# Weight pieces that begin 32 to 256 bytes into their buffers, with later attention steps and two half banks at the end

## The chip, the cores and the metric

The kernel runs on one NeuronCore of a Trainium2 chip (core 0). The metric is the device time of one execution in microseconds (us). Work is done by TensorE (PE in the profile; its loads of the stationary operand are listed apart as PEld), VectorE (DVE), ScalarE (ACT), and by DMAs that SyncE (SP) issues. GpSimd (POOL) only sets a few small buffers.

## The reference

A two-layer encoder trunk on 256 tokens of width 1024, in float32. Both layers sit between two half-step SwiGLU FFNs; the first mixes tokens by gated linear attention (GLA), the second by differential softmax attention.

```python
for i in range(2):
    x = x + 0.5 * swiglu_ffn(rms_norm(x, g[i, 0]), w_gu[i, 0], w_down[i, 0])
    h = rms_norm(x, g[i, 1])
    x = x + (gla_mixer(h, ...) if i == 0 else diff_mixer(h, ...))
    x = x + 0.5 * swiglu_ffn(rms_norm(x, g[i, 2]), w_gu[i, 1], w_down[i, 1])

def swiglu_ffn(h, w_gu, w_down):          # w_gu 1024 x 5632, w_down 2816 x 1024
    gate, up = jnp.split(h @ w_gu, 2, axis=-1)
    return (jax.nn.silu(gate) * up) @ w_down
```

The weights of the four FFNs, of the input and of the output projections are some 177 MB in all, read once.

## The kernel before

**Pieces of weights.** `weight_plan` lists all weights as 169 pieces of up to 1 MB, in the order in which they are used. A piece is loaded by one DMA into a staging buffer (`prefetch`), and then split by `parts` into a high and a low half (both float32r) that stand side by side in a buffer of the pool `wpool`: ACT copies the high half, DVE subtracts it from the staged weights to get the low half (line 186). There are five such buffers of 16 KB in each partition. The activations are split in the same way: `x2` (a normalized input), `a2` (the FFN's inner activation), `o2` and `do2` (outputs of the two mixers). A product is made as high times high, high times low and low times high.

**Which operand stands still.** In most products the weights are the stationary operand, 128 x 128 at a time, and the activation moves past them. Three helpers issue the matmuls:

- `mm3` (lines 210 and 211), for the FFNs: one matmul moves 512 columns (both halves of `x2` or `a2`) past the high weights, the next moves 256 columns past the low weights. Each pair of lines is a pair of matmuls with two loads. A gate or up projection is 11 chunks of 2 banks of 8 such pairs; the four FFNs make 4 x 11 x 2 x 2 x 8 = 1408 pairs on `x2`. The down projections of the first three FFNs make 3 x 4 x 2 x 22 = 528 pairs on `a2`.
- `mm1` (lines 203 to 205): three matmuls of 256 columns, for the GLA's q and k and for the output projections (`ps_w`).
- `mm_tok` (lines 225 to 227): the activation stands still and the weights move, mostly 512 columns at a time ("wide" pieces): the GLA's v and g, the differential layer's q, k and v, and the last FFN's down projection (`ps_d` on those lines).

**Where things lie.** In the build before, the five weight buffers begin at byte 42,400 of each partition and lie 16,384 bytes apart; `x2` begins at byte 132,512, the `a2` of the FFNs at 160,992 or 165,088, `o2` at 201,440 and `do2` at 162,016. Within each buffer every 128- or 256-column operand begins a multiple of 512 bytes further on. Modulo 512 bytes, then, a weight operand minus an `x2` operand is always 0, and a weight operand minus an operand of `a2`, `o2` or `do2` is always 192.

**The order of the differential layer** is written out by hand in the string `ORDER`. An `h` is a quarter or half of a projection (some 12 matmuls of 512 columns, or 24 of 256); between them stand the steps of head pair c: `b` statistics of q and k (`qk_stats`), `n` their scaling and transposition (`qk_norm`, tiles `qkx`, `ps_f`, `qkn`), `s` the softmax of one head (`ps_sc`, `s`), `f` the transposition of the probabilities (`flip`, `ps_T`, `dT`), `a` the product with v (`attend`, `ps_do`, `do`), `o` the transposition of the result (`normalize`, `ps_doT`). Each engine runs its own instructions in the order of the build.

**The end.** `down_out` makes the last down projection in two halves of 512 output columns, each of them in two banks of 128 tokens. In the very last bank, the last two of 22 blocks are done as two halves of 256 columns, so that DVE can add the first half to the residual (line 445) and SP can send it out (line 448) while the second is multiplied:

```python
if not whole:
    mm_tok(ps, w, act, t, k0, nk, hs, skip_group_check=h == 1)
nc.vector.scalar_tensor_tensor(out=xt[:, t, ho], in0=ps[:, hs], ...)
nc.sync.dma_start(out[0, ts_, ho], xt[:, t, ho])
```

Of the kernel before, what the change touches and what calls it, by code (L numbers as in the profile page):

```python
# [11 lines left out]
F32 = mybir.dt.float32  # L12
# [6 lines left out]
P = 128  # L19
# [11 lines left out]
WW, WK = 512, 4  # L31

N_STAGE = 3
WARM = 8
# [22 lines left out]
def weight_plan(w):  # L57

    plan = []

    def cols(a, start, width=CW, times=1):
        plan.append((a[:, start : start + width], KD, width, times))

    def wide(a, c, nk=KD):

        for k0 in range(0, nk, WK):
            n = min(WK, nk - k0)
            plan.append((a[k0 * P : (k0 + n) * P, c * WW : (c + 1) * WW], n, WW, 1))

    def both(a, b):  # L70

        for k0 in range(0, KD, WK):
            plan.append((tuple(z[k0 * P : (k0 + WK) * P, :CW] for z in (a, b)), WK, WW, 1))

    def ffn(i, j):
        gu, down = w["ffn_w_gu"][i, j], w["ffn_w_down"][i, j]
        for c in range(FF // CW):
            cols(gu, c * CW)
            cols(gu, FF + c * CW)
        if (i, j) == (1, 1):  # L80
            for c in range(D // WW):
                wide(down, c, NFB)
            return
        for dc in range(D // CW):
            for k0 in range(0, NFB, KD):
                n = min(KD, NFB - k0)
                plan.append((down[k0 * P : (k0 + n) * P, dc * CW : (dc + 1) * CW], n, CW, 1))

    ffn(0, 0)
    gla = w["gla_w_in"][0]  # L90

    cols(gla, gla.shape[1] - 32, 32, 4)
    for kind, c in GLA_COLS.split():
        if kind in "qk":
            cols(gla, "qk".index(kind) * 512 + int(c) * CW)
        else:
            wide(gla[:, 1024:], "vg".index(kind) * 2 + int(c))
    for c in range(4):
        cols(w["gla_w_out"][0], c * CW)
    ffn(0, 1)  # L100
    ffn(1, 0)
    for kind, c in DIFF_COLS.split():
        a, c = w["diff_w_in"][0], int(c)
        if kind == "a":
            both(a[:, c * CW :], a[:, D + c * CW :])
        elif kind == "b":
            wide(a[:, 2 * D :], c)
        else:
            cols(a, 2 * D + c * CW)
    for c in range(4):  # L110
        cols(w["diff_w_out"][0], c * CW)
    ffn(1, 1)
    return plan
# [3 lines left out]
def trunk(ctx: ExitStack, tc: tile.TileContext, ins, out):  # L117
# [19 lines left out]
    def prefetch(n):  # L137
        while state["dma"] < min(len(plan), n + LOOK_DMA + 1):
            i = state["dma"]
            src, nk, width, _ = plan[i]  # L140
            srcs = src if isinstance(src, tuple) else (src,)
# [10 lines left out]
    def parts():  # L152

        i = state["split"]
        _, nk, width, times = plan[i]
# [63 lines left out]

    def mm_tok(ps, w, act, t, k0, nk, cs=slice(None), **more):  # L220

        ts_ = slice(t * P, (t + 1) * P)
        for wk in range(w.shape[1]):
            k = k0 + wk
            mm(ps[:, cs], lhsT=act[:, k, 0, ts_], rhs=w[:, wk, 0, cs], start=k == 0, stop=False, **more)  # L225
            mm(ps[:, cs], lhsT=act[:, k, 0, ts_], rhs=w[:, wk, 1, cs], start=False, stop=False, **more)  # L226
            mm(ps[:, cs], lhsT=act[:, k, 1, ts_], rhs=w[:, wk, 0, cs], start=False, stop=k == nk - 1, **more)  # L227

# [197 lines left out]
    def down_out(act, nk, coef, xt):  # L426

        for c in range(D // WW):
            cs = slice(c * WW, (c + 1) * WW)
            banks = [psA.tile([P, WW], F32, tag="A", name=f"ps_d{c}_{t}") for t in range(2)]  # L430
            for k0 in range(0, nk, WK):
                w = next_weights()
                for t, ps in enumerate(banks):
                    if k0 + WK < nk:
                        mm_tok(ps, w, act, t, k0, nk)
                        continue

                    ts_, whole = slice(t * P, (t + 1) * P), t == 0 or c == 0
                    if whole:
                        mm_tok(ps, w, act, t, k0, nk)  # L440
                    for h in range(2):
                        hs, ho = slice(h * CW, (h + 1) * CW), slice(c * WW + h * CW, c * WW + (h + 1) * CW)
                        if not whole:
                            mm_tok(ps, w, act, t, k0, nk, hs, skip_group_check=h == 1)
                        nc.vector.scalar_tensor_tensor(  # L445
                            out=xt[:, t, ho], in0=ps[:, hs], scalar=coef, in1=xt[:, t, ho], op0=ALU.mult, op1=ALU.add,
                        )
                        nc.sync.dma_start(out[0, ts_, ho], xt[:, t, ho])

    def first_group():  # L450

        n = Norm(0)
        with ExitStack() as xctx:
            xp = xctx.enter_context(tc.tile_pool(name="xin", bufs=1))
            x_tm = xp.tile([P, 2, D], F32, name="x_tm")
            src, nk, width, _ = plan[0]
            t0 = staged[0] = stage.tile([P, nk, width], F32, tag="stage", name="stage0")
# [631 lines left out]
```

## Time and profile before

| | before |
|---|---|
| device time, median of 3 runs | 1006.99 us (1005.82 to 1007.09) |
| device time of the profiled execution | 1007.02 us |
| its span, first to last instruction | 1005.1 us |
| TensorE busy, as the profile counts it | 995.3 us (99%) |
| VectorE busy | 745.3 us (74%) |
| ScalarE busy | 566.1 us (56%) |
| HBM traffic | 177 GB/s over the span |

A matmul's length in the profile is modelled and overlaps the next one's; how long one holds up the next is read from the starts of two that follow each other. The profiled execution is within 0.1 us of the median of the runs, so that a sum made against it holds for the runs too.

### The profile page before, as it was taken

Reading aid. Unit: us, or ns where it says so; the run is one execution under the profiler, and the core shown is the slowest. Engines: PE = TensorE matmul, PEld = TensorE weight load, DVE = VectorE, ACT = ScalarE, POOL = GpSimd, SP = SyncE. Lnnn points to the kernel's source line nnn. Section 1 sums busy time; section 2 is a strip of 40 time slices with the busy share of each in tenths; the row PEclk is TensorE's granted clock in tenths of the full one; section 3 lists DMA queues with packets and bytes.
Section 4 is the critical chain, followed back from the end, with each engine's and each line's share of the span. In section 5 each row is a group of like instructions: output and inputs, shape, how many; then the busy total and the mean of one; then the engine's idle time right before and its main releaser. Section 6 shows DMA issues by size and latency. Waiting matters only on the chain.

```text
span 1005.1 us, 14771 instructions
## 1 busy us (share of the span) xinstructions
PE 995.3 (99%) x5830; PEld 870.4 (87%) x5830; DVE 745.3 (74%) x1275; ACT 566.1 (56%) x946; POOL 1.4 (0%) x9
## 2 busy tenths in 40 slices
PE   8999999999999999999999999999999999999998
PEld 7888888898889888888888888888878998888886
DVE  6988756499977987774669787556989689777640
ACT  6756545298655765553456565435586576655430
POOL 0000000000000000000000000000000000000000
PEclk9999999999999999999999999999999999999999
DMA  9876453565322775655457565465663258655530
GB/s 285 262 234 201 160 186 121 171 218 196 127 84 84 252 250 170 197 158 178 158 182 257 176 201 165 140 224 160 205 203 103 67 194 272 204 168 186 171 126 22
DMA packets 166787, 178.87 MB, mean 178 GB/s; under 512 B 4579, under 2 KB 155550, under 8 KB 166718
## 3 DMA queue, kind: packets, MB, share of 16 engines
q1 hardware_dynamic: 166318, 177.71, 54.7%
q8 instruction: 46, 0.75, 0.3%
q10 hardware_dynamic: 400, 0.21, 0.1%
q14 instruction: 23, 0.19, 0.1%
HBM read 176.84 MB, written 1.06 MB: 177 GB/s over the span
## 4 chain that ended last, share of the span: by engine, by line
PE 68%; DVE 5%; ACT 2%; issue 1%; ACTq 0%
PE ps_u L210 12%; PE ps_g L210 12%; PE ps_d L210 8%; PE ps_g L211 6%; PE ps_u L211 6%; PE ps_d L211 4%; PE ps_d L225 2%; PE ps_d L227 2%; PE ps_d L226 2%; DVE w L186 2%; PE ps_s L677 1%; PE ps_w L203 1%; PE ps_w L204 1%; PE ps_w L205 1%; ACT w L186 1%; PE ps_g L225 1%
## 5 line engine op out<-in xcount | busy, mean ns | idle before, releaser
L186 DVE TENSOR_TENSOR w<-stage,w 128x1024 fp32r<-128x1024 f32 x332 | 384.3, 1197 | 35.4 <-ACT w L186 35.2
L186 ACT ACTIVATE w<-stage 128x1024 fp32r<-128x1024 f32 x332 | 327.0, 1035 | 53.4 <-PE ps_d L227 15.3
L210 PE MATMUL ps_g<-x,w 128*128 128x512 f32 x704 | 250.6, 398 | 0.9 <-ACT w L502 0.9
L210 PE MATMUL ps_u<-x,w 128*128 128x512 f32 x704 | 249.1, 396 | 0.0
L211 PE MATMUL ps_g<-x,w 128*128 128x256 f32 x704 | 197.7, 282 | 0.0
L211 PE MATMUL ps_u<-x,w 128*128 128x256 f32 x704 | 197.5, 280 | 0.0
L210 PE MATMUL ps_d<-a,w 128*128 128x512 f32 x528 | 186.7, 396 | 0.0
L210 PEld LDWEIGHTS ps_g<-x,w 128*128 128x128 f32 x704 | 132.5, 189 | 32.8 <-ACT w L502 1.2
L210 PEld LDWEIGHTS ps_u<-x,w 128*128 128x128 f32 x704 | 132.1, 188 | 31.2
L211 PE MATMUL ps_d<-a,w 128*128 128x256 f32 x528 | 148.9, 282 | 0.0
L211 PEld LDWEIGHTS ps_g<-x,w 128*128 128x128 f32 x704 | 133.5, 190 | 0.2
L211 PEld LDWEIGHTS ps_u<-x,w 128*128 128x128 f32 x704 | 133.0, 189 | 0.0
L210 PEld LDWEIGHTS ps_d<-a,w 128*128 128x128 f32 x528 | 99.2, 188 | 24.0
L211 PEld LDWEIGHTS ps_d<-a,w 128*128 128x128 f32 x528 | 99.2, 188 | 0.0
L321 ACT ACTIVATE x<-x,par 128x256 fp32r<-128x256 f32 x40 | 20.0, 506 | 119.8 <-DVE x L374 119.8
L250 ACT COPY half<-ps_u 128x256 f32<-128x256 f32 x88 | 32.8, 372 | 90.4 <-PE ps_u L211 88.4
L250 ACT COPY half<-ps_g 128x256 f32<-128x256 f32 x88 | 32.3, 371 | 83.1 <-PE ps_g L211 81.5
L251 DVE TENSOR_TENSOR up<-ps_u,half 128x256 f32<-128x256 f32 x88 | 36.8, 421 | 40.4 <-ACT half L250 40.3
L374 DVE SCALAR_TENSOR_TENSOR x<-ps_d,x 128x256 f32<-128x256 f32 x48 | 20.3, 423 | 61.0 <-PE ps_d L211 60.1
L251 DVE TENSOR_TENSOR gate<-ps_g,half 128x256 f32<-128x256 f32 x88 | 36.8, 421 | 38.3 <-ACT half L250 38.3
L225 PE MATMUL ps_d<-w,a 128*128 128x512 f32 (+1 forms) x90 | 35.2, 391 | 0.5 <-DVE xt L445 0.5
L226 PE MATMUL ps_d<-w,a 128*128 128x512 f32 (+1 forms) x90 | 35.1, 390 | 0.0
(241 smaller groups left out, 1331.7 us busy)
## 6 DMA issues: line engine op xcount, KB each, us to landing
stage<-in_ffn_w_gu_dram SPq DMA_DIRECT2D x86, 1024.0 KB, 5.2
stage<-in_ffn_w_down_dram SPq DMA_DIRECT2D x34, 1024.0 KB, 5.3
stage<-in_gla_w_in_dram SPq DMA_DIRECT2D x12, 1024.0 KB, 7.6
stage<-in_ffn_w_down_dram SPq DMA_DIRECT2D x12, 768.0 KB, 4.5
stage<-in_diff_w_in_dram SPq DMA_DIRECT2D x16, 512.0 KB, 4.7
stage<-in_gla_w_out_dram SPq DMA_DIRECT2D x4, 1024.0 KB, 5.7
stage<-in_diff_w_in_dram SPq DMA_DIRECT2D x4, 1024.0 KB
stage<-in_diff_w_out_dram SPq DMA_DIRECT2D x4, 1024.0 KB, 5.5
```

The source lines that it names most:

```text
L186: op()
L203: mm(ps, lhsT=w[:, k, 0, ms], rhs=act[:, k, 0, :], start=first, stop=False)
L204: mm(ps, lhsT=w[:, k, 0, ms], rhs=act[:, k, 1, :], start=False, stop=False)
L210: mm(ps, lhsT=w[:, wk, 0, ms], rhs=act[:, k, :, :], start=first, stop=False)
L211: mm(ps[:, 0:T], lhsT=w[:, wk, 1, ms], rhs=act[:, k, 0, :], start=False, stop=last)
L225: mm(ps[:, cs], lhsT=act[:, k, 0, ts_], rhs=w[:, wk, 0, cs], start=k == 0, stop=False, **more)
L226: mm(ps[:, cs], lhsT=act[:, k, 0, ts_], rhs=w[:, wk, 1, cs], start=False, stop=False, **more)
L227: mm(ps[:, cs], lhsT=act[:, k, 1, ts_], rhs=w[:, wk, 0, cs], start=False, stop=k == nk - 1, **more)
L250: nc.scalar.copy(h[:, b, :], ps[:, T:512])
L251: nc.vector.tensor_tensor(out=out_t[:, b, :], in0=ps[:, 0:T], in1=h[:, b, :], op=ALU.add)
L321: high = nc.scalar.activation(self.x2[:, d, 0, :], src, AF.Copy, scale=g)
L374: nc.vector.scalar_tensor_tensor(out=x[:, d, :], in0=ps[:, h * T : (h + 1) * T], scalar=coef, in1=x[:, d, :], op0=ALU.mult, op1=ALU.add,)
```

## The change

Four things change.

1. A buffer of `wpool` becomes 16,896 bytes, and a piece begins at an offset in it that depends on how it is used: 24 elements (96 bytes) for weights that stand still beside `x2`, 8 (32 bytes) beside `a2`, `o2` or `do2`, 64 (256 bytes) for wide pieces that move past `x2`, 16 (64 bytes) for those that move past `a2`. The two narrow v pieces of the differential layer (256 columns, which also move past `x2`) get 96 bytes. The size and number of all splits and weight loads stay the same.
2. The memory kept for DMA descriptors shrinks from 16 KB to 8 KB in each partition, which makes room for the larger buffers.
3. In `ORDER`, twelve steps stand one quarter later (`n0`, `b1`, `n1`, `f0`, `s10`, `s11`, `a0`, `n2`, `s20`, `s21`, `a1`, `f2`) and two more stand two quarters later (`f1`, `o0`); the other ten stay (`s00` and `s01`, for one, now follow `n0` after one quarter where it was two).
4. In `down_out`, the very last bank becomes two tiles of 256 columns for all 22 blocks.

In the build after, the weight buffers begin at byte 34,208 and lie 16,896 bytes (33 x 512) apart; `x2` begins at 126,880, `a2` at 155,360 or 159,456, `o2` at 195,808 and `do2` at 156,384. Modulo 512 bytes the difference of a weight operand and the activation that it meets is:

| | before | after |
|---|---|---|
| weights stand still, `x2` moves | 0 | 96 |
| weights stand still, `a2`, `o2` or `do2` moves | 192 | 224 |
| wide weights move past `x2` | 0 | 256 |
| wide weights move past `a2` | 192 | 256 |

```diff
+BESIDE_X, BESIDE_A, WIDE_X, WIDE_A = 24, 8, 64, 16
+W_PAD = 128
...
-h h h h h h b0 h h n0 b1 h h s00 s01 n1 h h h f0 h s10 s11 h h f1 b2 a0 n2 h s20 s21 o0 h a1 h h b3 h f2 h n3 o1 a2 s30 s31 h h o2 hold
+h h h h h h b0 h h h n0 b1 h s00 s01 h n1 h h h f0 h s10 s11 h b2 h n2 a0 h f1 s20 s21 h a1 o0 h b3 h h f2 n3 o1 a2 s30 s31 h h o2 hold
...
-        w = split[i] = wpool.tile([P, nk, 2, times * width], FR, tag="w", name=f"w{i}")
+        n = nk * 2 * times * width
+        whole = wpool.tile([P, 2 * KD * CW + W_PAD], FR, tag="w", name=f"w{i}")
+        w = split[i] = whole[:, shift : shift + n].rearrange("p (k h c) -> p k h c", h=2, c=times * width)
...
-            banks = [psA.tile([P, WW], F32, tag="A", name=f"ps_d{c}_{t}") for t in range(2)]
+            banks = [[psA.tile([P, WW], F32, tag="A", name=f"ps_d{c}_{t}")] for t in range(2)]
+            if c == D // WW - 1:
+                banks[1] = [psA.tile([P, CW], F32, tag="A", name=f"ps_d{c}_1_{h}") for h in range(2)]
...
-    nc = bacc.Bacc("TRN2", target_bir_lowering=False, num_devices=1)
+    nc = bacc.Bacc("TRN2", target_bir_lowering=False, num_devices=1, dynamic_dma_scratch_size=8192)
```

What the steps look like on TensorE, at three places. First, the transposition of head pair 0's probabilities (`ps_T0`, `ps_T1`) in the middle of the differential layer's v projection (`ps_db0_0`, first token block). Before:

```order
L227 MATMUL ps_db0_0_6802<-w125_6537,x2_4_5895 128x512
L955 MATMUL ps_T0_6816<-cst_81,s0_0_6701 128x128 x4
L225 MATMUL ps_db0_0_6802<-w126_6646,x2_4_5895 128x512
L226 MATMUL ps_db0_0_6802<-w126_6646,x2_4_5895 128x512
L227 MATMUL ps_db0_0_6802<-w126_6646,x2_4_5895 128x512
L225 MATMUL ps_db0_0_6802<-w126_6646,x2_4_5895 128x512
L955 MATMUL ps_T1_6822<-cst_81,s1_0_6734 128x128
L226 MATMUL ps_db0_0_6802<-w126_6646,x2_4_5895 128x512
L955 MATMUL ps_T1_6822<-cst_81,s1_0_6734 128x128 x3
L227 MATMUL ps_db0_0_6802<-w126_6646,x2_4_5895 128x512
```

After (all lines of the file are 4 to 6 further on; the `ps_db0_0` group above ends before them):

```order
L232 MATMUL ps_db0_0_6802<-w126_6610,x2_4_5895 128x512
L233 MATMUL ps_db0_0_6802<-w126_6610,x2_4_5895 128x512
L231 MATMUL ps_db0_0_6802<-w126_6610,x2_4_5895 128x512
L232 MATMUL ps_db0_0_6802<-w126_6610,x2_4_5895 128x512
L233 MATMUL ps_db0_0_6802<-w126_6610,x2_4_5895 128x512
L959 MATMUL ps_T0_6837<-cst_81,s0_0_6701 128x128 x4
L959 MATMUL ps_T1_6843<-cst_81,s1_0_6734 128x128 x4
L231 MATMUL ps_db0_1_6849<-w125_6537,x2_4_5895 128x512
```

The transpositions stood between the two quarters of `ps_db0_0` and stand behind the second one now. Second, the product of head pair 1 with v (`ps_do1`) and the transposition of head pair 0's result (`ps_doT0`), between quarters of the last q and k projection (`ps_da3`). Before:

```order
L226 MATMUL ps_da3_0_7030<-w128_6797,x2_4_5895 128x512
L227 MATMUL ps_da3_0_7030<-w128_6797,x2_4_5895 128x512
L989 MATMUL ps_do1_7138<-dv_tm0_6847,dT1_6940 128x128 x2
L1006 MATMUL ps_doT0_7108<-cst_81,do_7006 128x128 x4
L989 MATMUL ps_do1_7138<-dv_tm0_6847,dT1_6940 128x128 x6
L225 MATMUL ps_da3_1_7172<-w127_6666,x2_4_5895 128x512
L226 MATMUL ps_da3_1_7172<-w127_6666,x2_4_5895 128x512
```

After, behind the next quarter's matmuls, and with all of `ps_do1` ahead of `ps_doT0`:

```order
L232 MATMUL ps_da3_1_7131<-w127_6666,x2_4_5895 128x512
L233 MATMUL ps_da3_1_7131<-w127_6666,x2_4_5895 128x512
L993 MATMUL ps_do1_7144<-dv_tm0_6834,dT1_7053 128x128 x8
L1010 MATMUL ps_doT0_7178<-cst_81,do_7028 128x128 x4
L231 MATMUL ps_da3_1_7131<-w128_6797,x2_4_5895 128x512
L232 MATMUL ps_da3_1_7131<-w128_6797,x2_4_5895 128x512
```

Here the transposition has moved back by two quarters and the product by one. Third, the end of the program, where `ps_d1_1` is the last bank. Before:

```order
L225 MATMUL ps_d1_0_9159<-w168_9221,a2_7817 128x512
L226 MATMUL ps_d1_0_9159<-w168_9221,a2_7817 128x512
L227 MATMUL ps_d1_0_9159<-w168_9221,a2_7817 128x512
L225 MATMUL ps_d1_1_9160<-w168_9221,a2_7817 128x256
L226 MATMUL ps_d1_1_9160<-w168_9221,a2_7817 128x256
L227 MATMUL ps_d1_1_9160<-w168_9221,a2_7817 128x256
L225 MATMUL ps_d1_1_9160<-w168_9221,a2_7817 128x256
L226 MATMUL ps_d1_1_9160<-w168_9221,a2_7817 128x256
L227 MATMUL ps_d1_1_9160<-w168_9221,a2_7817 128x256
L225 MATMUL ps_d1_1_9160<-w168_9221,a2_7817 128x256
L226 MATMUL ps_d1_1_9160<-w168_9221,a2_7817 128x256
L227 MATMUL ps_d1_1_9160<-w168_9221,a2_7817 128x256
```

After:

```order
L231 MATMUL ps_d1_0_9159<-w168_9247,a2_7817 128x512
L232 MATMUL ps_d1_0_9159<-w168_9247,a2_7817 128x512
L233 MATMUL ps_d1_0_9159<-w168_9247,a2_7817 128x512
L231 MATMUL ps_d1_1_0_9161<-w168_9247,a2_7817 128x256
L232 MATMUL ps_d1_1_0_9161<-w168_9247,a2_7817 128x256
L233 MATMUL ps_d1_1_0_9161<-w168_9247,a2_7817 128x256
L231 MATMUL ps_d1_1_0_9161<-w168_9247,a2_7817 128x256
L232 MATMUL ps_d1_1_0_9161<-w168_9247,a2_7817 128x256
L233 MATMUL ps_d1_1_0_9161<-w168_9247,a2_7817 128x256
L231 MATMUL ps_d1_1_1_9162<-w168_9247,a2_7817 128x256
L232 MATMUL ps_d1_1_1_9162<-w168_9247,a2_7817 128x256
L233 MATMUL ps_d1_1_1_9162<-w168_9247,a2_7817 128x256
```

The 256-column matmuls of the last two blocks write two tiles where they wrote halves of one. Ahead of this place, the 60 matmuls of 512 columns that filled `ps_d1_1` from the other 20 blocks are 120 of 256 columns now.

## Rows read from the trace of the kernel before

**Rows 1.** The page of the profile: its span and busy times of the engines.
```profile
span 1005.1 us, 14771 instructions
PE 995.3 (99%) x5830; PEld 870.4 (87%) x5830; DVE 745.3 (74%) x1275; ACT 566.1 (56%) x946; POOL 1.4 (0%) x9
```

**Rows 2.** Groups of instructions by line; columns as in the page's part 5.
```profile
L210 PE MATMUL ps_g<-x,w 128*128 128x512 f32 x704 | 250.6, 398 | 0.9 <-ACT w L502 0.9
...
L210 PE MATMUL ps_d<-a,w 128*128 128x512 f32 x528 | 186.7, 396 | 0.0
```

**Rows 3.** Timeline of PE, first FFN: start, length, what.
```profile
30.06 0.39 PE L210 MATMUL ps_u<-x,w 128*128 128x512 f32 x1
30.29 0.28 PE L211 MATMUL ps_u<-x,w 128*128 128x256 f32 x1
...
32.14 0.39 PE L210 MATMUL ps_u<-x,w 128*128 128x512 f32 x1
```

**Rows 4.** Timeline of PE, later in the same FFN.
```profile
99.50 0.28 PE L211 MATMUL ps_u<-x,w 128*128 128x256 f32 x1
99.61 0.40 PE L210 MATMUL ps_u<-x,w 128*128 128x512 f32 x1
...
99.96 0.40 PE L210 MATMUL ps_u<-x,w 128*128 128x512 f32 x1
...
100.32 0.40 PE L210 MATMUL ps_u<-x,w 128*128 128x512 f32 x1
...
102.79 0.40 PE L210 MATMUL ps_u<-x,w 128*128 128x512 f32 x1
```

**Rows 5.** Windows, line 210 alone: stretch, length, PE busy (count), PEld, clock, DMA.
```profile
340.00:440.00 100.00, 100.00 (x284) 53.17 (x283) 1.00 0.64 207
512.00:632.00 120.00, 119.37 (x344) 64.16 (x343) 1.00 0.61 198
895.00:935.00 40.00, 39.11 (x113) 21.14 (x113) 1.00 0.52 175
```

**Rows 6.** Timeline of PE, differential layer, weights moving past x2.
```profile
730.06 0.39 PE L226 MATMUL ps_da<-w,x 128*128 128x512 f32 x1
...
731.65 0.39 PE L227 MATMUL ps_da<-w,x 128*128 128x512 f32 x1
```

**Rows 7.** Timeline of PE, last down projection, weights moving past a2.
```profile
970.16 0.39 PE L225 MATMUL ps_d<-w,a 128*128 128x512 f32 x1
...
971.79 0.40 PE L226 MATMUL ps_d<-w,a 128*128 128x512 f32 x1
```

**Rows 8.** Timeline of PE, output projection of the differential layer.
```profile
806.01 0.28 PE L203 MATMUL ps_w<-do,w 128*128 128x256 f32 x1
...
807.43 0.28 PE L203 MATMUL ps_w<-do,w 128*128 128x256 f32 x1
```

**Rows 9.** Waits of PE in the differential layer: total us, times, longest.
```profile
PE ps_doT L1006 <- DVE do L998: 1.7, 2, 1.0
PE ps_T L955 <- DVE s L944: 0.4, 1, 0.4
...
PE ps_db L225 <- DVE mx L928: 0.3, 1, 0.3
```

**Rows 10.** Windows, all engines: stretch, length, busy (count) of each, clock, DMA.
```profile
700.00:750.00 50.00, 48.76 (x262) 39.22 (x261) 47.84 (x144) 34.28 (x67) 0.00 (x0) 1.00 0.70 222
750.00:800.00 50.00, 48.24 (x380) 44.74 (x380) 36.95 (x141) 30.14 (x91) 0.00 (x0) 1.00 0.26 85
```

**Rows 11.** Timeline of the end, all engines.
```profile
999.76 1.11 DVE L445 SCALAR_TENSOR_TENSOR xt<-ps_d,xt 128x256 f32<-128x256 f32 x3 [21.48 <-PE ps_d L227]
...
1000.14 0.28 PE L227 MATMUL ps_d<-w,a 128*128 128x256 f32 x1
...
1000.93 0.19 PEld L225 LDWEIGHTS ps_d<-w,a 128*128 128x128 f32 x1 [0.71 <-DVE xt L445]
```

**Rows 12.** The page's DMA queues.
```profile
q1 hardware_dynamic: 166318, 177.71, 54.7%
```

More of the change, by code (lines that the diff above doesn't have):

```diff
@@ L59, in weight_plan, with cols, wide @@
     plan = []
-    def cols(a, start, width=CW, times=1):
-        plan.append((a[:, start : start + width], KD, width, times))
-    def wide(a, c, nk=KD):
+    def cols(a, start, width=CW, times=1, shift=BESIDE_X):
+        plan.append((a[:, start : start + width], KD, width, times, shift))
+    def wide(a, c, nk=KD, shift=WIDE_X):
         for k0 in range(0, nk, WK):
             n = min(WK, nk - k0)
-            plan.append((a[k0 * P : (k0 + n) * P, c * WW : (c + 1) * WW], n, WW, 1))
+            plan.append((a[k0 * P : (k0 + n) * P, c * WW : (c + 1) * WW], n, WW, 1, shift))
     def both(a, b):
         for k0 in range(0, KD, WK):
-            plan.append((tuple(z[k0 * P : (k0 + WK) * P, :CW] for z in (a, b)), WK, WW, 1))
+            plan.append((tuple(z[k0 * P : (k0 + WK) * P, :CW] for z in (a, b)), WK, WW, 1, WIDE_X))
     def ffn(i, j):
@@ L81, in ffn @@
             for c in range(D // WW):
-                wide(down, c, NFB)
+                wide(down, c, NFB, WIDE_A)
             return
@@ L86, in ffn @@
                 n = min(KD, NFB - k0)
-                plan.append((down[k0 * P : (k0 + n) * P, dc * CW : (dc + 1) * CW], n, CW, 1))
+                plan.append((down[k0 * P : (k0 + n) * P, dc * CW : (dc + 1) * CW], n, CW, 1, BESIDE_A))
     ffn(0, 0)
@@ L154, in parts @@
         i = state["split"]
[L155 removed]
+        _, nk, width, times, shift = plan[i]
         t = staged.pop(i)
[L157 removed]
+        n = nk * 2 * times * width
+        whole = wpool.tile([P, 2 * KD * CW + W_PAD], FR, tag="w", name=f"w{i}")
+        w = split[i] = whole[:, shift : shift + n].rearrange("p (k h c) -> p k h c", h=2, c=times * width)
         state["split"] += 1
@@ L218, in project, with mm_tok @@
         return banks
-    def mm_tok(ps, w, act, t, k0, nk, cs=slice(None), **more):
+    def mm_tok(ps, w, act, t, k0, nk, cs=slice(None)):
         ts_ = slice(t * P, (t + 1) * P)
@@ L224, in mm_tok @@
             k = k0 + wk
-            mm(ps[:, cs], lhsT=act[:, k, 0, ts_], rhs=w[:, wk, 0, cs], start=k == 0, stop=False, **more)
-            mm(ps[:, cs], lhsT=act[:, k, 0, ts_], rhs=w[:, wk, 1, cs], start=False, stop=False, **more)
-            mm(ps[:, cs], lhsT=act[:, k, 1, ts_], rhs=w[:, wk, 0, cs], start=False, stop=k == nk - 1, **more)
+            mm(ps, lhsT=act[:, k, 0, ts_], rhs=w[:, wk, 0, cs], start=k == 0, stop=False)
+            mm(ps, lhsT=act[:, k, 0, ts_], rhs=w[:, wk, 1, cs], start=False, stop=False)
+            mm(ps, lhsT=act[:, k, 1, ts_], rhs=w[:, wk, 0, cs], start=False, stop=k == nk - 1)
     class Wide:
@@ L428, in down_out @@
         for c in range(D // WW):
-            cs = slice(c * WW, (c + 1) * WW)
-            banks = [psA.tile([P, WW], F32, tag="A", name=f"ps_d{c}_{t}") for t in range(2)]
+            banks = [[psA.tile([P, WW], F32, tag="A", name=f"ps_d{c}_{t}")] for t in range(2)]
+            if c == D // WW - 1:
+                banks[1] = [psA.tile([P, CW], F32, tag="A", name=f"ps_d{c}_1_{h}") for h in range(2)]
             for k0 in range(0, nk, WK):
                 w = next_weights()
[L433 to L448, printed above, removed]
+                for t, tiles in enumerate(banks):
+                    ts_, n = slice(t * P, (t + 1) * P), WW // len(tiles)
+                    for i, ps in enumerate(tiles):
+                        mm_tok(ps, w, act, t, k0, nk, slice(i * n, (i + 1) * n))
+                        if k0 + WK < nk:
+                            continue
+                        for h in range(0, n, CW):
+                            ho = slice(c * WW + i * n + h, c * WW + i * n + h + CW)
+                            nc.vector.scalar_tensor_tensor(
+                                out=xt[:, t, ho], in0=ps[:, h : h + CW], scalar=coef, in1=xt[:, t, ho], op0=ALU.mult, op1=ALU.add,
+                            )
+                            nc.sync.dma_start(out[0, ts_, ho], xt[:, t, ho])
     def first_group():
```

8 lines of the change are left out of this document (4 added, 4 removed).

## The prediction

> **What bounds the kernel now.** I read the page first: TensorE is busy for 995.3 of 1005.1 us, VectorE for 745.3, ScalarE for 566.1 [rows 1]. Since a matmul's length is modelled and overlaps the next, "99% busy" only says that TensorE hardly ever waits for others. So the question is how fast its matmuls follow each other, and for that the view is the timeline, by the starts of two that follow each other. By count most of them are the pairs of lines 210 and 211: 704 for the gates, as many for the ups, and 528 for the first three down projections [rows 2].
>
> The timeline shows two paces for the same pair on the same operands. Around 30 us six pairs take from 30.06 to 32.14 us, 346.7 ns each [rows 3]. Around 100 us nine pairs take from 99.61 to 102.79 us, 353.3 ns each, and there the pace goes round in three: two pairs that stand beside each other in the rows take 0.35 and 0.36 us [rows 4]. Both paces are kept for long. The windows show 284 pairs in 100 us (the slow pace), and 344 in 119.4 and 113 in 39.1 us (the quick one) [rows 5]. The clock column is 1.00 throughout, the upper level (2.4 GHz), so the clock is not what differs. Where the operands change places, the pace depends on what is met: seven matmuls of 512 columns past `x2` take 1.59 us, 227 ns each [rows 6]; seven past `a2` take 1.63 us, 233 ns each [rows 7]. The steps are alike: 353.3 to 346.7 and 233 to 227 are both 6.7 ns. Twelve matmuls of 256 columns take 1.42 us, 118 ns each [rows 8].
>
> What the reader is to see: TensorE's stream runs at paces a fixed step apart, at a clock that does not move, and one of the things that goes with the pace is which buffers meet. In this kernel weights and `x2` lie 0 bytes apart modulo 512, and weights and `a2` 192. That the address is the cause is not shown: `a2` and `x2` differ in more than that, and one set of addresses goes at two paces [rows 3, 4].
>
> **The change part by part.**
>
> *Offsets, weights standing still.* No instruction is added; the price is a change of pace times a count. The nearest rows give the bounds. The slow pace is 353.3, the quick one 346.7. One more step down is 340; that is also what the quickest single matmuls in the rows add up to, 227 ns of 512 columns [rows 6] and one of 256 columns that is followed after 0.11 us [rows 4]. One step up is 360, the longest pair of rows 4. I take 340, since it needs nothing that the rows don't show somewhere, and since 0 and 192 bytes are only two of many offsets, and already give paces a step apart. Of the 1408 pairs on `x2`, the quick stretches hold 344 + 113 = 457 [rows 5]; I count the other 951 as slow. That gives 951 x 13.3 = 12.7 us and 457 x 6.7 = 3.0 us. The 528 pairs on `a2` are at the slow pace: 528 x 13.3 = 7.0 us. Together 22.7 us. Nothing hides this, nor takes it back: in the FFNs no other engine is late, and faster matmuls come out of the span one for one as long as VectorE (74%) keeps up.
>
> *Offsets, weights moving.* 198 matmuls of 512 columns past `a2` remain in the last down projection (3 x 66 of its four banks' 264; the fourth bank is cut up). From 233 to 227 ns they give 198 x 6.7 = 1.3 us. Those past `x2` are at 227 already, the quickest in the rows, and I leave them there (another step would be 6.7 ns on 192 of them in the GLA, 1.3 us). The 256-column matmuls I leave at 118 too.
>
> A rule of the Trainium skill speaks against all of this. The page "TensorE: Matmul & The Clock Gate", section "Step-by-step: what each phase is for", says that TensorE has two independent read ports to SBUF, one for the moving operand and one for weight loads, and that loading the next weights doesn't take read bandwidth from the running matmul. By it the place of the weights can't matter, and the offsets would give 0 in place of 24 us. The trace does not bear it out fully: the same shape at the same clock differs by 6.7 ns with the operand [rows 6, 7]. The section "Back-to-back issue gap" of that page of the Trainium skill gives N / 2.4 + 2.5 ns, which would make 325 ns of a pair; no row here is that quick, and by it the whole sum would be 29 us larger for the pairs alone (an estimate from that section of the Trainium skill).
>
> *Steps of the differential layer.* The named waits of TensorE there are 1.7 us for `do` (the longer of the two is 1.0), 0.4 for `s` and 0.3 for `mx` [rows 9]. The 0.7 us of `do` that is left belongs to the output projection, which isn't changed; at most 1.7 us is to be had, and by waits that move elsewhere nothing. Behind each of these waits stand the projection's matmuls, in TensorE's order. But VectorE is busy for 47.84 of 50 us from 700 to 750 [rows 10], and steps that come later on TensorE don't lessen its work; from 750 it has 13 us free, so what is moved there fits. I take 1.0 us. For the same reason a faster TensorE buys little in this stage: matmuls on `x2` there have no share in my sum.
>
> *Half banks at the end.* Before, the load for the second half waits 0.71 us until VectorE has read the first half of the same tile [rows 11]; with two tiles it need not. Against it stand 120 matmuls of 256 columns for 60 of 512: 120 x 118 - 60 x 233 = 0.2 us. Net 0.5 us off the last chain, with only the last addition and store behind it.
>
> *Less descriptor memory.* The 177.71 MB go through one hardware queue [rows 12] and GpSimd does almost nothing [rows 1]; I cost it at 0. If the smaller ring made loads late, ScalarE's copies would wait first, and TensorE soon after, since pieces are split only three ahead. Writes of the split to shifted places I cost at 0 too: VectorE and ScalarE have slack outside 700 to 750 us.
>
> Sum: 22.7 + 1.3 + 1.0 + 0.5 = 25.5 us off the profiled execution's 1007.0 (which is the median of the runs): 981.5 us.
>
> **The rivals.**
>
> *R1, only the quick pace.* The new offsets lock the stream into the pace that it already finds by chance: 951 + 528 pairs gain 6.7 ns each, 9.9 us, plus 1.3 + 1.5: 994 us. For it: 346.7 is the quickest pace that lasts in the rows. Against it: single matmuls are quicker than their mean in it.
>
> *R2, more than one step.* Pairs at 333 (another 6.7 x 1936 = 12.9 us) and wide matmuls at 220 (198 + 192 of them, 2.6 us): 966 us, and further steps beyond, to 950. For it: the steps are even, and nothing shows that 340 is the last. Against it: no row has such matmuls.
>
> *R3, the offset does nothing.* The pace is set by how a stream starts, as one address with two paces suggests [rows 3, 4]: 1007.0 - 1.5 = 1005.5 us. The rule of the Trainium skill on the two ports would give the same time.
>
> *R4, slower.* 96 bytes puts the stream one step up in the FFNs: 360 in place of 353.3 or 346.7 for the pairs on `x2`, 951 x 6.7 + 457 x 13.3 = 12.4 us: 1007.0 - 1.5 + 12.4 = 1018 us. It decides as soon as the pairs' pace is above about 353 on the mean. For it: differences of 0 and 192 show the better and the worse of two paces, and which one 96 gives can't be read.
>
> **How the numbers follow.** The forecast (340) 0.30, R1 0.24, R2 0.22, R3 0.12, R4 0.12. The predicted time is the forecast's, 981. The range from 958 to 1005 holds the forecast, R1, most of R2 and R3, and leaves out R4 and the far end of R2, about 2 in 10. A measurement of this kernel can tell about 0.2%, 2 us, from no change. Faster by more than that: the forecast, R1, R2 and a quarter of R3, 0.79; within it: the rest of R3, 0.09; slower: R4, 0.12.
>
> **What would show it.** In the timeline of the FFNs, pairs at one pace throughout, 340 ns (346.7: R1; 333 or less: R2; 346.7 and 353.3 mixed as before: R3; 360: R4). Wide matmuls past `a2` at 227. No wait for `do` near the last q and k projection, and no load that waits for `xt` at the end. I would be wrong if the paces came from something that the offset does not touch, such as where the accumulators lie, or if a faster TensorE ran into VectorE outside the differential layer: then waits for `w` would stand in TensorE's view.

## The result and the profile after

| | before | after |
|---|---|---|
| device time, median | 1007.04 us (1005.82 to 1007.32, 4 runs) | 996.14 us (994.58 to 996.36, 4 runs) |
| profiled execution, span | 1007.02, 1005.1 us | 995.94, 994.1 us |

The ratio is 0.9891, with a 95% interval from 0.9874 to 0.9908: faster by 11 us, where 25.5 had been forecast. Rival R1 (994 us) came out.

The page of the changed kernel answers to [rows 1]: TensorE is as busy as before, in a shorter span, and the other engines have the same work.

```profile
span 994.1 us, 14886 instructions
PE 983.7 (99%) x5890; PEld 871.5 (88%) x5890; DVE 745.6 (75%) x1275; ACT 565.3 (57%) x946; POOL 1.4 (0%) x9
```

The timeline of TensorE at the place of [rows 4] (start, length, what; lines 216 and 217 were 210 and 211):

```profile
99.92 0.39 PE L216 MATMUL ps_u<-x,w 128*128 128x512 f32 x1
100.15 0.28 PE L217 MATMUL ps_u<-x,w 128*128 128x256 f32 x1
100.26 0.39 PE L216 MATMUL ps_u<-x,w 128*128 128x512 f32 x1
...
100.61 0.39 PE L216 MATMUL ps_u<-x,w 128*128 128x512 f32 x1
...
102.69 0.39 PE L216 MATMUL ps_g<-x,w 128*128 128x512 f32 x1
```

Eight pairs from 99.92 to 102.69, 346.7 ns each, and every pair like the next: the round of three is gone. The windows of line 216 show the same over long stretches (length, PE busy and count, weight loads, clock, DMA):

```profile
340.00:440.00 100.00, 100.00 (x289) 54.14 (x289) 1.00 0.64 205
512.00:632.00 120.00, 119.68 (x346) 64.72 (x345) 1.00 0.63 201
```

The first window held 284 pairs before [rows 5] and holds 289 now; the second, which was at the quick pace already, stays at it. On `a2`, the window from 140 to 190 us with the same fields, before and after:

```profile
140.00:190.00 50.00, 50.00 (x142) 26.55 (x142) 1.00 0.47 144
140.00:190.00 50.00, 50.00 (x145) 27.08 (x145) 1.00 0.54 168
```

Over all pairs whose starts the timelines give, a pair on `x2` took 350.7 ns on the mean before and takes 346.7, a pair on `a2` 353.3 and takes 346.7. So the change found the quick pace of [rows 3] and put all pairs into it, and none went below.

Wide weights past `a2` took 233 ns [rows 7]; the timeline of the last down projection now has seven in 1.59 us, 227 ns each:

```profile
955.02 0.39 PE L231 MATMUL ps_d<-w,a 128*128 128x512 f32 x1
...
956.61 0.39 PE L232 MATMUL ps_d<-w,a 128*128 128x512 f32 x1
```

The matmuls of 256 columns that fill the last two half banks go at 120 ns, fifteen in 1.80 us:

```profile
986.05 0.28 PE L231 MATMUL ps_d<-w,a 128*128 128x256 f32 x1
...
987.85 0.40 PE L231 MATMUL ps_d<-w,a 128*128 128x512 f32 x1
```

The waits of TensorE from 690 to 800 us, for [rows 9] (total us, times, longest):

```profile
PE ps_sc L925 <- DVE qkx L900: 1.8, 2, 0.9
PE ps_da L231 <- DVE do L1002: 1.1, 1, 1.1
PE ps_doT L1010 <- DVE do L1002: 0.7, 1, 0.7
PE ps_f L908 <- ACT dT L960: 0.2, 1, 0.2
```

They sum to 3.8 us; before they were 2.8, the three of [rows 9] and 0.4 for `qkx`. The waits for `do` and `s` ahead of the moved steps went, as intended, and the scores `ps_sc` now wait for `qkx`, and a projection (`ps_da`) for `do`: VectorE is as busy as before, and TensorE only meets it elsewhere.

### The profile page after: what moved, and what is told of

It reads as the page before. It is cut to its first block, busy times and chain, and to the rows that moved or that the text cites. A ratio compares the mean times of both kernels' runs of the same rounds, so it can differ in the third digit from the quotient of the medians.

```text
span 994.1 us, 14886 instructions
## 1 busy us (share of the span) xinstructions
PE 983.7 (99%) x5890; PEld 871.5 (88%) x5890; DVE 745.6 (75%) x1275; ACT 565.3 (57%) x946; POOL 1.4 (0%) x9
## 4 chain that ended last, share of the span: by engine, by line
PE 69%; DVE 4%; ACT 2%; issue 1%; DMA 0%; SPq 0%; ACTq 0%
PE ps_u L216 12%; PE ps_g L216 12%; PE ps_d L216 8%; PE ps_g L217 6%; PE ps_u L217 6%; PE ps_d L217 4%; PE ps_d L232 2%; PE ps_d L231 2%; PE ps_d L233 2%; DVE w L192 2%; PE ps_s L681 1%; PE ps_w L209 1%; PE ps_w L210 1%; PE ps_w L211 1%; PE ps_g L231 1%; PE ps_g L233 1%
## 5 line engine op out<-in xcount | busy, mean ns | idle before, releaser
L216 PE MATMUL ps_g<-x,w 128*128 128x512 f32 x704 | 246.6, 392 | 0.8 <-ACT w L506 0.8
L216 PE MATMUL ps_u<-x,w 128*128 128x512 f32 x704 | 246.3, 392 | 0.0
L216 PE MATMUL ps_d<-a,w 128*128 128x512 f32 x528 | 183.2, 390 | 0.0
L232 PE MATMUL ps_d<-w,a 128*128 128x512 f32 (+1 forms) x110 | 38.2, 347 | 0.0
L231 PE MATMUL ps_d<-w,a 128*128 128x512 f32 (+1 forms) x110 | 38.2, 347 | 0.0
```

What stands on the lines that cost most here:

```text
L216: mm(ps, lhsT=w[:, wk, 0, ms], rhs=act[:, k, :, :], start=first, stop=False)
L231: mm(ps, lhsT=act[:, k, 0, ts_], rhs=w[:, wk, 0, cs], start=k == 0, stop=False)
L232: mm(ps, lhsT=act[:, k, 0, ts_], rhs=w[:, wk, 1, cs], start=False, stop=False)
```

## The experiments

The theory after the result (P): the pace of a pair is set by where its operands lie, and the offsets alone gave the gain. Its rivals (Q): the other parts of the change gave it, or the way in which the stream starts sets the pace. What the quickest pace is, and whether another offset reaches it, was the second question.

All times are medians of device time; a ratio is against the kernel before on the same chip. A pair's pace is worked out as the spacing of the starts of two 512-column matmuls of `mm3` that follow each other. "Difference" is the byte address of the weight operand minus that of the activation that it meets, modulo 256 unless said otherwise.

**1. Only the offsets** (the order of the steps and the last bank as before; the larger buffers and the 8 KB for descriptors stay as changed):

```diff
 (the change, without these two parts)
-h h h h h h b0 h h h n0 b1 h s00 s01 h n1 ...
+h h h h h h b0 h h n0 b1 h h s00 s01 n1 ...
-                banks[1] = [psA.tile([P, CW], F32, tag="A", name=f"ps_d{c}_1_{h}") for h in range(2)]
```

> The kernel before with the offsets and the larger buffers alone (old order of the differential layer, old last bank). Theory P (the offset decides the pace of the pairs): all pairs at 346.7 ns in the FFNs, wide matmuls past a2 at 227, and about 995.5 to 997 us, since 1479 slow pairs give 9.9 us and the wide ones 1.3. Theory Q (the gain comes from the later steps and the half banks, and the quick pace in the changed kernel is a chance of how its streams start): pairs at two paces as before, 1004 to 1007 us.

Measured: 994.49 us (993.44 to 995.14, 4 runs), ratio 0.9876 [0.9861, 0.9891]. All pairs at 346.7. The offsets alone give all of the gain. The view of waits, same stretch as above:

```profile
PE ps_doT L1012 <- DVE do L1004: 1.7, 2, 1.0
PE ps_T L961 <- DVE s L950: 0.4, 1, 0.4
PE ps_db L231 <- DVE mx L934: 0.3, 1, 0.3
PE ps_f L910 <- DVE qkx L902: 0.2, 1, 0.2
```

2.6 us of waits with the old order, 3.8 with the new one. The differential stage, from its first matmul to the first of the output projection, takes 91.0 us here (686.2 to 777.2) and 91.8 in the changed kernel (686.4 to 778.2).

**2. The change without offsets:**

```diff
-BESIDE_X, BESIDE_A, WIDE_X, WIDE_A = 24, 8, 64, 16
+BESIDE_X, BESIDE_A, WIDE_X, WIDE_A = 0, 0, 0, 0
```

> The changed kernel with all four offsets at 0, all else as changed (larger buffers, less descriptor memory, later steps, half banks). Theory P: pairs on a2 at 353.3, those on x2 at 353.3 for most of the time, wide ones past a2 at 233, and 1005 to 1007 us: the later steps and the half banks are worth under 2 us. Theory Q: pairs at 346.7 and 995 to 997 us.

Measured: 1005.19 us (1004.63 to 1007.7, 10 runs), ratio 0.9987 [0.9977, 0.9996]. Pairs on `x2` 350.8 ns on the mean, on `a2` 353.3, wide matmuls past `a2` 233.3: the three as before. With all the other parts of the change in place, larger buffers and less descriptor memory among them, it is nearly the kernel before.

**3. A sweep of offsets**, each piece 32 bytes further than the one before it, 0 to 480 and back:

```diff
-    return plan
+        n = seen[shift] = seen.get(shift, -1) + 1
+        turn, at = divmod(n, 16)
+        swept.append((src, nk, width, times, 8 * (at if turn % 2 == 0 else 15 - at)))
+    return swept
```

> The changed kernel, but the offset goes up by 32 bytes from piece to piece (0 to 480 bytes, then down again), by itself for each of the four kinds. Each piece of a gate or up projection is 16 pairs, so one run shows the pace at all sixteen offsets, reached from below and from above. Theory P: a pace that belongs to the offset, the same on both passes and in all FFNs; 346.7 at differences 96 and 224, 353.3 at 0 and 192. It doesn't say whether any offset gives 340. Theory Q: no pattern by offset; the pace is kept from piece to piece.

Measured: 1004.08 us (one run). The timeline at a border between two pieces, 96 bytes of difference up to 574.08, 64 from there on, line 221 only:

```profile
572.00 0.39 PE L221 MATMUL ps_u<-x,w 128*128 128x512 f32 x1
...
573.73 0.39 PE L221 MATMUL ps_u<-x,w 128*128 128x512 f32 x1
...
574.77 0.40 PE L221 MATMUL ps_g<-x,w 128*128 128x512 f32 x1
...
576.89 0.40 PE L221 MATMUL ps_g<-x,w 128*128 128x512 f32 x1
```

Five pairs from 572.00 to 573.73 are 346 ns each; six from 574.77 to 576.89 are 353 each. Same buffer of `x2`, same loop, and the pace turns with the offset of the weights. The steady paces, without the first pairs of a piece:

| difference | 0 | 32 | 64 | 96 | 128 | 160 | 192 | 224 |
|---|---|---|---|---|---|---|---|---|
| ns a pair | 353.3 | 353.3 (once 346.8) | 353.3 | **346.7** | 351.2 | 350.1 | 353.3 | **346.7** |

The table holds for `x2` and `a2` alike, on the way up and down, and repeats at 256 bytes (352 is like 96, 480 like 224). So 96 and 224, the change's choice, are the two quickest of eight. At a difference of 0 the pairs go round in three, 349, 350 and 361 ns: the rounds of [rows 4]; at 32 they take 346 and 361 by turns. For 0 the table has only the slower of two paces: the kernel before and experiment 2 also keep 346.7 there for whole stages. Wide matmuls past `a2` are at 226.7 where the difference is 0 or 256 modulo 512, near 229 at 64 and 320, and at 233 and above elsewhere. Matmuls of 256 columns were quickest, 113.3 once steady, where the address of the moving operand is 192 above that of the stationary one, modulo 256, and 120.0 at 0: the half banks of the change meet at 256.

**4. Weights at 0, `x2` moved instead** (by 416 bytes, so that the difference is 96 again; `a2` is back at 192):

```diff
-BESIDE_X, BESIDE_A, WIDE_X, WIDE_A = 24, 8, 64, 16
+BESIDE_X, BESIDE_A, WIDE_X, WIDE_A = 0, 0, 0, 0
-            self.x2 = xpool.tile([P, KD, 2, T], FR, tag="x2", name=f"x2_{idx}")
+            whole = xpool.tile([P, KD * 2 * T + 128], FR, tag="x2", name=f"x2_{idx}")
+            self.x2 = whole[:, 104 : 104 + KD * 2 * T].rearrange("p (k h t) -> p k h t", h=2, t=T)
```

> The changed kernel with the weights at offset 0, and x2 begun 416 bytes on in a larger buffer, so that weights minus x2 is 96 modulo 512 while the weights lie where they lay in the kernel before. If the difference of the two addresses is what counts (theory P): pairs on x2 at 346.7, pairs on a2 at 353.3 (192 as before), about 999 us. If it is where the weights themselves begin within 64 or 512 bytes (theory W): pairs on x2 at the two paces of before, 1005 us or more.

Measured: 1000.22 us (one run). The windows of line 216, first `x2`, then `a2`:

```profile
340.00:440.00 100.00, 100.00 (x289) 54.09 (x289) 1.00 0.63 205
450.00:490.00 40.00, 40.00 (x114) 21.23 (x113) 1.00 0.54 179
```

289 pairs on `x2`, as with the change; 114 on `a2`, where the changed kernel has 117 in the same window. The pace follows the difference of the two addresses, not the place of the weights. One thing was not expected: in the first FFN the pairs on `a2` ran at 349 and not at 353.3, so a difference of 192 has a second pace too.

**5. A finer sweep**, 16 bytes a step on `x2`, 4 on `a2` (192 to 256):

```diff
+        swept.append((src, nk, width, times, at + 1 if shift == BESIDE_A else 4 * at))
```

> The changed kernel with offsets that go up in steps of 16 bytes (0 to 240, then down) for the pieces that meet x2, and in steps of 4 bytes (4 to 64, then down) for those whose pairs meet a2, which there makes differences of 196 to 256 bytes. The sweep in steps of 32 bytes found 346.7 ns as the quickest pace of a pair, at 96 and 224 bytes alone. Theory F (346.7 is the floor of this pair at any place): no piece below 346.7; quick places in a band around 96 and 224. Theory G (a finer place is quicker, the forecast's 340): some offset that is no multiple of 32 gives 340 or less.

Measured: 1004.93 us (one run). On `x2`, 346.7 at 16, 48, 96 and 224, 353.3 at 0 (but 347 in the first piece of all), 64, 80, 112, 192 and 240, both at 32, and 349 to 351 at the others (176 twice at 353.5). On `a2`, 346.3 to 346.8 at 196, 204, 232 and 244. Nothing is below 346.3: for a single offset, 346.3 to 346.8 is the quickest pace that any offset tried gives.

**6. The best of the sweeps together**: offsets, the old order, the 256-column products at the difference of 113 ns, and both last banks as half banks.

```diff
-        cols(w["gla_w_out"][0], c * CW, shift=BESIDE_A)
+        cols(w["gla_w_out"][0], c * CW, shift=32)
...
-                wide(down, c, NFB, WIDE_A)
+                wide(down, c, NFB, (WIDE_A, 0)[c])
...
+            n = WW if c == 0 else CW
+            banks = [[psA.tile([P, n], F32, tag="A", name=f"ps_d{c}_{t}_{h}") for h in range(WW // n)] for t in range(2)]
```

> The offsets with the old order of the differential layer, and two things that the sweep points to: matmuls of 256 columns, which come in the sweep every 113.3 to 113.8 ns where the moving operand lies 192 bytes on from the stationary one (modulo 256), get offsets for that (the q, k, v and output projections), and the last 512 output columns are four tiles of 256 columns at that offset in place of one bank and two half banks. If the sweep's paces hold outside it: 384 x 3 to 4 ns and 192 x 5 ns, some 2.3 us, and half a us at the end, below the 994.5 us of the offsets alone: 991 to 992 us. If a pace in the sweep depends on what ran before: 994 to 995 us.

Measured: 994.98 us (994.31 to 995.71, 4 runs), ratio 0.9885 [0.9866, 0.9905]: no better than the offsets alone. The 256-column matmuls past `a2` ran at 117.8 and not at 113.3, though experiment 2 has them at 113.3 at the same difference. The output projections went in part at 113.3 and in part at 117.8, 116 to 117.5 on the mean. At one difference these matmuls have two paces, and most stayed in the slower.

**7. The change with the old order of the steps:**

```diff
-h h h h h h b0 h h h n0 b1 h s00 s01 h n1 ...
+h h h h h h b0 h h n0 b1 h h s00 s01 n1 ...
```

> The changed kernel with the order of the differential layer from before; offsets and half banks as changed. If the later steps are what cost the changed kernel its loss against the offsets alone (the layer took 91.8 us with them and 91.0 without): 995.2 us, the rest of that loss (0.1 to 0.8 us) being the half banks at 120 ns a matmul. If the later steps help, as I forecast: 997 us.

Measured: 995.54 us (994.01 to 996.42, 4 runs), ratio 0.9892 [0.9873, 0.991]. By the whole time it can't be told from the changed kernel; by its trace the differential stage takes 91.0 us (686.3 to 777.3) in place of 91.8, with the same waits as in experiment 1.

**8. Two offsets**: the high and the low weights of a piece begin at offsets of their own, in all 64 combinations of steps of 32 bytes.

```diff
-        whole = wpool.tile([P, 2 * KD * CW + W_PAD], FR, tag="w", name=f"w{i}")
-        w = split[i] = whole[:, shift : shift + n].rearrange("p (k h c) -> p k h c", h=2, c=times * width)
+        whole = wpool.tile([P, 2, KD * CW + W_PAD // 2], FR, tag="w", name=f"w{i}")
+        w = split[i] = Parts(*(
+            whole[:, h, s : s + n].rearrange("p (k c) -> p k c", c=times * width) for h, s in enumerate(shift)
+        ))
...
+        swept.append((src, nk, width, times, (8 * (n % 8), 8 * (n // 8 % 8))))
```

> The changed kernel, but the high and the low halves of a piece stand in two parts of the buffer, each with its own offset; from piece to piece the pair of offsets goes through 8 x 8 combinations (0 to 224 bytes each, in steps of 32). The load of the low weights runs beside 512 moving columns, that of the high weights beside 256. Alone, 512 columns are quickest at a difference of 0 or 256 (226.7 ns) and 256 columns at 64 (113.3). Theory H (the forecast's 340 can be had, when each load has the place that suits what moves beside it): a combination of high 64 and low 0 gives 340, and others lie between 340 and 360. Theory F (346.7 is the floor of this pair): no combination below 346.7.

Measured: 1001.91 us (one run). Most combinations lie between 346.5 and 354. Three were below for a piece or more (difference of high, difference of low): (224, 0) 344 in two pieces, (96, 32) 343 in two pieces and 352 in one, (192, 0) 350 in two and 340 to 342 in one. This is the last, the first down projection piece of its FFN:

```profile
444.30 0.39 PE L233 MATMUL ps_d<-a,w 128*128 128x512 f32 x1
...
448.38 0.39 PE L233 MATMUL ps_d<-a,w 128*128 128x512 f32 x1
```

Twelve pairs in 4.08 us, 340 ns each: the pace that the prediction had named, but at offsets that the change doesn't use. The pair that theory H had named for it, (64, 0), ran at 350 in all three of its pieces.

**9, 10, 11. These three pairs of offsets, held through the kernel**, on the basis of experiment 1 (values in elements, high and low):

```diff
-BESIDE_X, BESIDE_A, WIDE_X, WIDE_A = 24, 8, 64, 16
+BESIDE_X, BESIDE_A, WIDE_X, WIDE_A = (56, 0), (8, 16), (64, 64), (16, 16)
```

That is (224, 0); (24, 8), (40, 24) stand there for (96, 32), and (48, 0), (0, 16) for (192, 0).

> The offsets alone (old order, old last bank), but the high and the low weights of a piece begin at different offsets: high weights minus moving operand 224 bytes modulo 256, low weights minus moving operand 0, for x2 and for a2, o2 and do2; wide pieces as in the change. In the map of two offsets both passages of such a piece ran at 344 ns a pair. Theory H (two offsets have a pace of their own, and it lasts): some 1930 pairs at 344 instead of 346.7, 5 us less than the offsets alone, 989 to 990 us. Theory F (346.7 is the quickest pace that lasts, and the 344 came from the change between two pieces): 994.5, and pairs at 346.7 or slower in the trace.

> As before with high weights minus moving operand 96 bytes modulo 256 and low weights minus moving operand 32. The map had such pieces at 343 twice and at 352 once. Theory H with one pace: 1930 pairs at 343, 7 us less than the offsets alone, 987.5 us. If it has two paces, as offset 32 alone had, and what ran before decides: pieces at 343 and at 352 in one trace, and a time between 987 and 1004. Theory F: 994.5.

> As before with high weights minus moving operand 192 bytes modulo 256 and low weights minus moving operand 0. The map had such pieces at 350, 340 and 350. Theory H with two paces: pieces at 340 and at 350 in one trace; all at 340 would give 1930 x 6.7 = 13 us less than the offsets alone, 981.5, all at 350 6 us more, 1000.9. Theory F: the 340 does not return, and the time is that of 350, 1000 to 1001.

| | time | ratio | pairs on `x2` | on `a2` |
|---|---|---|---|---|
| (224, 0) | 996.06 us (995.26 to 996.77) | 0.9907 [0.9893, 0.9922] | 344 at first, 353 from 46 to 136 us and for a piece near the start of later stages, else 347 | 346.7 |
| (96, 32) | 992.48 us (991.04 to 993.52) | 0.9872 [0.9855, 0.9888] | 352 to 135 us and for a piece or two at the start of later stages, else 343 | 352 in the first FFN, then 343 |
| (192, 0) | 989.13 us (986.48 to 989.94) | 0.9834 [0.9818, 0.985] | 340, but 350 from 45 to 135 us and from 875 us to the end of that stage | 340.1 |

For (224, 0) theory F held: its 344 stayed for two pieces and gave way to 353 and 347. By its ratio (96, 32) can't be told from the offsets alone (0.9876); (192, 0) is quicker than they are. The trace of (192, 0) is of the quickest of its four runs, 986.48 us; what the others did is not shown. Both have two paces that last, and where one turns into the other something stands in between. In the kernel of (192, 0), the timeline at 45 us:

```profile
43.16 0.39 PE L229 MATMUL ps_u<-x,w 128*128 128x512 f32 x1
...
43.84 0.39 PE L229 MATMUL ps_u<-x,w 128*128 128x512 f32 x1
44.06 0.28 PE L230 MATMUL ps_u<-x,w 128*128 128x256 f32 x1
44.27 0.22 PE L312 MATMUL ps_rows<-cst,rows 5*128 5x5 f32 x1
44.42 1.02 PE L858 MATMUL ps_rel<-oh,tab 32*8 32x512 f32 x2
...
45.83 0.40 PE L229 MATMUL ps_g<-x,w 128*128 128x512 f32 x1
...
46.53 0.40 PE L229 MATMUL ps_g<-x,w 128*128 128x512 f32 x1
```

Two pairs in 0.68 us ahead of `ps_rows` and `ps_rel` (340 each), two in 0.70 behind them (350 each), and so on to the end of that stage. The other turn, at 874 us, follows the transpositions of the residual (`ps_xt`).

**12. These breaks moved** to the last chunk of their stages, otherwise the kernel of (192, 0):

```diff
-                if first and c == 3:
+                if first and c == FF // CW - 1:
...
-                if nxt is None and c == 6:
+                if nxt is None and c == FF // CW - 1:
```

> As the two offsets of 192 and 0, but with the small matmuls that stood inside the first gate and up stage (the transposed parameters and the float32 table of relative positions, between its pieces 6 and 7) and inside the last one (the transposed residual, behind its piece 13) moved to the last chunk of the stage. In the kernel before it, the pairs ran at 340 ns up to these places and at 350 behind them, to the end of the stage. Theory B (a break by other matmuls decides anew which of the two paces runs, and without one a pace lasts): both stages keep 340 up to their last chunk, some 13 and 7 more pieces of 16 pairs, 320 x 10 ns = 3.2 us less, 983 to 986 us. Rival: the pace changes with the buffer that a piece lies in, with time, or with the transfers that run beside it; then 350 comes back at the same places, and the time stays at 986.5 to 990.

Measured: 982.45 us (981.38 to 984.97, 5 runs), ratio 0.9767 [0.975, 0.9784]. The timeline ahead of and behind the break at its new place:

```profile
99.65 0.39 PE L229 MATMUL ps_g<-x,w 128*128 128x512 f32 x1
...
100.67 0.39 PE L229 MATMUL ps_g<-x,w 128*128 128x512 f32 x1
...
119.95 1.02 PE L858 MATMUL ps_rel<-oh,tab 32*8 32x512 f32 x2
...
121.36 0.40 PE L229 MATMUL ps_g<-x,w 128*128 128x512 f32 x1
...
121.71 0.40 PE L229 MATMUL ps_g<-x,w 128*128 128x512 f32 x1
```

Three pairs from 99.65 to 100.67 are 340 each, where the kernel of experiment 11 ran at 350; behind the break, 350 is back. In the last gate and up stage all pieces keep 340 to 342. Over the kernel a pair on `x2` takes 340.4 ns and one on `a2` 340.1. Theory B holds, and its rival (buffers, time or transfers) falls: the same buffers and transfers pass at nearly the same times. This is the quickest kernel of all: some 24 us less than before, where the change gave 11. Its span is 4.1 us below that of experiment 11, 980.5 to 984.6; 3.2 had been expected. The ratios differ by more, 0.9834 to 0.9767, some 6.7 us; what the runs of experiment 11 without a trace lost beyond the 4.1 is open.

## Why the prediction was wrong

**The failed step** is "I take 340" for the pairs. It added up the quickest single spacings of different streams, 227 of [rows 6] and 0.11 of [rows 4], and took the sum for a pace. The round of three in [rows 4] said otherwise: there a quick pair is paid for by a slow one right behind it, and only the mean over the round counts. Experiments 3 and 5 show what one offset can do: 346.7 at best, and eight offsets of 32 bytes give 346.7, 350, 351 and 353, not a ladder of even steps. A pair at 340 does exist, but only where the high and the low weights have differences of their own (experiments 8, 11 and 12). The term was 22.7 us; by the trace it is 1408 x (350.7 - 346.7) + 528 x (353.3 - 346.7) = 5.6 + 3.5 = 9.1 us. R1, which counted one step where the forecast counted one or two, has 9.9 there, because it took 951 pairs on `x2` for slow ones in full.

**What was right.** That the pace depends on how the addresses lie, and that faster matmuls come out of the span one for one: shown by experiments 1 to 4. The prediction had left open whether the address is the cause; it is, and it is the difference that counts. It does not decide alone: at some differences two paces last (see R3 below), and at 96 and 224 none but 346.7 did.

A page of the Trainium skill, "TensorE: Matmul & The Clock Gate", section "Step-by-step: what each phase is for", gives TensorE two independent read ports, so that loading the next weights takes no read bandwidth from the running matmul. If that were all, the place of the weights would not matter; experiments 3 and 4 speak against it for these matmuls, 346.7 or 353.3 by the difference of the addresses, at a granted clock of 1.00. By the formula for an isolated matmul in the section "Back-to-back issue gap" of that page of the Trainium skill a pair would take 325 ns (an estimate); the quickest that lasts in any run here is 340.

**Wide past `a2`**, forecast 1.3 us: 198 x (233.3 - 227.5) = 1.1. They are at 226.7 but for the first five behind each group of half-bank matmuls, which take 228 to 236; in experiment 1, without the half banks, the mean is 226.7.

**Later steps**, forecast a gain of 1.0 us: a loss of 0.8, from 91.0 (experiment 7) to 91.8. The eight traces with the old order have 91.0 to 91.2 us for the stage, the six with the new one 91.8 to 92.2. The step that failed is that at least part of the 1.7 us would be had. The prediction had seen that VectorE is full from 700 to 750 us [rows 10]; it followed that a wait ended by VectorE only moves. The waits went from `do` and `s` to `qkx` and to `do` further on.

**Half banks**, forecast 0.5 us: the load's wait for `xt` (0.71 in [rows 11], 0.5 in TensorE's waits of experiment 1) is gone from the waits of the changed kernel and of experiment 7. But the 120 matmuls take 120.0 ns and not 118: 14.4 us, against 60 x 226.7 = 13.6 for the 512-column ones at the new offset. From the first to the last matmul of the last down projection, experiment 1 (old bank) takes 60.6 us, 928.96 to 989.54, and experiment 7 takes 60.7, 928.97 to 989.68: about nothing is gained, or a little lost. The forecast had priced the alternative at 233, which the offsets had just made quicker. At the old difference of the addresses (experiment 2) the same half banks took 113.3 ns a matmul, so the wide offset, which was right for 512 columns, was the wrong one for them, though that old difference does not assure 113.3 either (117.8 in experiment 6).

**Descriptor memory**, forecast 0: experiment 2 has it, with the larger buffers, and its ratio is 0.9987. TensorE waits for `w` once, 0.8 us in the changed kernel and 0.9 before.

The rest of the 11 us is small and not forecast: by the starts of the stages, the first FFN's matmuls begin 0.6 us earlier (8.8 in place of 9.4 us), which may be chance, since the other traces spread from 8.7 to 9.5, and the GLA takes 0.4 us less.

**Of the other rivals**, R3 (the pace is set by how a stream starts) is false as a whole and right in a part: at some differences two paces last, and what went before decides between them (experiments 11 and 12). A difference of 0 is one of these, and the trace of the kernel before turns at the same two breaks as that of experiment 11:

```profile
43.92 0.39 PE L210 MATMUL ps_u<-x,w 128*128 128x512 f32 x1
...
44.96 0.39 PE L210 MATMUL ps_u<-x,w 128*128 128x512 f32 x1
...
45.56 1.02 PE L839 MATMUL ps_rel<-oh,tab 32*8 32x512 f32 x2
...
46.96 0.40 PE L210 MATMUL ps_g<-x,w 128*128 128x512 f32 x1
...
50.14 0.40 PE L210 MATMUL ps_g<-x,w 128*128 128x512 f32 x1
```

Three pairs in 1.04 us ahead of `ps_rel`, 346.7 each; nine in 3.18 us behind it, 353.3 each. At the transpositions of the residual (`ps_xt`, from 893.02 us) it is the other way round: seven in 2.47 us ahead, 353 each, and eight in 2.77 behind the last of them, 346 each. Experiment 2 turns at both places too. This is why one address had two paces in [rows 3, 4]. With the change the pairs on `x2` are at 346.7 on both sides of these breaks. That a break is the cause was tested by moving it only for (192, 0); for the kernel before it is read from the place of the turns. R2 (333 or less) appeared at no offset tried, and R4 (360) at none, on the mean.

## What to carry to other kernels

When matmuls of the same shape run at two paces under one clock, sweep the difference of the two operands' addresses within one kernel, a piece at a time, before you trust any offset; and predict with the mean over the whole round of a stream, never with its quickest spacing. Sweep the operands of a pair apart too (the high and the low weights here): that is where the next step lay. Then hold the quick pace: keep other small matmuls out of a long stream, and test a pace that a sweep showed for one piece over the whole kernel, since of three such paces one did not last and the other two came beside a slower one. A wait that is ended by a full engine isn't removed by moving the step that waits.

## What the runs showed of the hardware

- The pace of a stream of float32r pairs depends on the difference of the addresses of the stationary and the moving operand, with a period of 256 bytes: 346.7 to 353.3 ns a pair with one offset, 340 to 353 with two. For single 512-column matmuls 226.7 to some 234, for 256-column ones 113.3 to 120.0.
- At some differences two paces last, 346.7 and 353.3 at 0 (the kernel before, experiment 2) and at 32, 349 and 353.3 at 192 (experiment 4), 340 and 350 at (192, 0), 343 and 352 at (96, 32), 113.3 and 117.8 for 256-column matmuls. At 96 and 224 only 346.7 was seen, in the changed kernel and in experiments 1, 3, 6 and 7. A break by other matmuls can turn one into the other, and the pace then lasts to the next break or the end of the stage, 90 us from 45 us on in the kernel before and in experiment 11.
- Why the difference matters, and what in a break decides, the runs don't show; nor do they show whether another pair of offsets than the 64 tried is below 340.
